# Contiguous places in memory for the triangular 64-blocks of a gated DeltaNet layer

## The chip, the cores and the metric

The kernel runs on one core of one Trainium2 chip. The metric is the device time of one launch in microseconds (us). The core has five engines that matter here: TensorE (PE, matrix products), VectorE (DVE), ScalarE (ACT), GpSimd (POOL) and SyncE (SP, which only issues transfers), and 16 DMA engines that all of them share.

## What is computed

One inference step of two layers for 512 prompt tokens and 8 sample tokens, width 2048. Layer 0 is a convolution module beside stick-breaking attention, layer 1 a gated DeltaNet with 16 query/key heads and 32 value heads of width 128. For the prompt, the DeltaNet works on chunks of 64 tokens. Per value head and chunk a unit lower triangular 64 x 64 matrix must be inverted:

```python
lmat = jnp.where(strict, jnp.einsum('bhnid,bhnjd->bhnij', kb, kc) * decay, 0.0)
tmat = lax.linalg.triangular_solve(lmat + eye, jnp.broadcast_to(eye, lmat.shape),
                                   left_side=True, lower=True, unit_diagonal=True)
u_val = tmat @ (vc * bc[..., None])
w_key = tmat @ (kb * jnp.exp(gc)[..., None])
...
def step(s, xs):
    u_n, w_n, qd_n, kd_n, a_n, gl_n = xs
    v_new = u_n - w_n @ s
    o_n = qd_n @ s + a_n @ v_new
    s = s * gl_n[..., None, None] + jnp.swapaxes(kd_n, -1, -2) @ v_new
    return s, o_n
```

## The kernel before, in words

The kernel handles the prompt in chunks of 128 tokens, so there are four chunks, and each holds two of the reference's 64-chunks. `build` (line 499) runs layer 0 first and then layer 1. Layer 1 has two stages that the change touches, and both stream the weights of the input projection through PE (`gemm`, `weights`): a block of 512 KB is loaded (`wr`, three buffers), split into a high part by ACT (`wh`) and a low part by DVE (`wl`), and multiplied.

The *preparing stage* calls `prepare(i)` (line 1307) for 16 head pairs i, some 26 us each. Each makes, for four chunks, seven 128 x 128 matrices and stores them in the DRAM tile `sp` (`spa`, line 1249; `spill[i]` is the part of head pair i): rows 0 and 1 the keys and queries, 2 the keys transposed, 3 and 4 the decayed products of both heads, and 5 and 6 the triangular matrices (`lt`) of both heads. These last two hold, on their diagonal, the two 64-blocks that have to be inverted. Then gates of some heads (`z`) are computed and stored.

`inverses(b8, iv)` (line 1377) inverts the blocks of eight head pairs at a time. The tile `m` has 128 partitions, one block of 64 x 64 on each, 2 MB in all. Eight transfers on Pool's queue (`Q2`) gather the blocks from `sp`, 16 partitions each, in rows of 64 numbers; DVE inverts them in place in some 238 operations; eight transfers scatter them back into the same places of `sp`. `inverses(0)` runs while head pairs 8 to 15 are prepared, the first half of its `m` being loaded once head pairs 0 to 3 are there. `inverses(1)` uses the same buffer for `m` and runs beside scans 0 to 7 of the next stage, in portions that `background` (line 1516) hands out.

The *scan stage* calls, for each head pair, `values(i)` (two projections and their convolution), `scan(i, ...)` (line 1594), `samples` and `normalise`. A scan loads its four chunks from `sp` into `pk` (four buffers, SP's queue), combines the two inverted 64-blocks of each head into the inverse of the 128-block with small products on PE, and runs the four steps of the recurrence.

The order of instructions on each engine is fixed by a planner, `Sched`. Every operation is recorded with its dependencies (`region`, line 120, finds out which parts of a tile two operations share) and a cost (`cost`, line 243); `flush` (line 309) simulates the engines and emits the instructions in the order of simulated start times. Pool's transfers (`GQ`) and Pool's own operations (`POOL`) are two engines for the planner but share one queue on the chip. The only operations of Pool in these stages, besides transfers, are memsets of three columns of `buf`, which the convolution (`conv_c`, line 1279) needs before ACT copies a projection from PSUM into `buf`. For a transfer the planner adds an issue time and the time of its bytes on one shared queue (lines 274, 275 and 401 to 404): 1700 ns of issue where a tile has at most 16 partitions, otherwise 340 or 560 ns, and bytes / 335 ns with a surcharge for short rows.

Of the kernel before, what the change touches and what calls it, by code (L numbers as in the profile page):

```python
# [8 lines left out]
F32 = mybir.dt.float32  # L9
# [6 lines left out]
P = 128  # L16
# [11 lines left out]
GQ = 16  # L28
# [10 lines left out]
class Sched:  # L39
# [80 lines left out]
    def region(self, ap):  # L120
        rec = self.owner.get(ap.tensor.name)
        if rec is None:
            return None
        dims, off = tuple(tuple(x) for x in ap.ap), ap.offset
        if ap.space == bass.MemoryType.DRAM:
            lo = off + sum(min(0, s * (c - 1)) for s, c in dims)
            hi = off + sum(max(0, s * (c - 1)) for s, c in dims)
            return rec, lo, hi + 1, self.parts(rec["shape"], dims, off) if len(rec["shape"]) == 4 else 1
        if ap.space == bass.MemoryType.PSUM:
            return rec, 0, P, 1  # L130
        fs = 1
        for x in rec["shape"][1:]:
            fs *= x
        key = (off % fs, dims[1:])
        m = self.masks.get(key)
        if m is None:
            idx = np.array([off % fs])
            for s, c in dims[1:]:
                if s:
                    idx = (idx[:, None] + s * np.arange(c)[None, :]).reshape(-1)  # L140
            b = np.zeros(idx.max() + 1, np.uint8)
            b[idx] = 1
            m = self.masks[key] = int.from_bytes(np.packbits(b, bitorder="little").tobytes(), "little")
        p0 = off // fs
        return rec, p0, p0 + dims[0][1], m
# [97 lines left out]
    def cost(self, eng, meth, args, kw, out, ins):  # L243

        n = self.free(out)
        PSM = bass.MemoryType.PSUM
        big = [x for x in ins if not (self.free(x) == 1 and n > 1)]
        ptr = len(ins) - len(big)
        nps = sum(1 for x in ins if x.space == PSM)
        acc = kw.get("accum_out") is not None  # L250
        if eng == "PE":
            k, m = ins[0].shape[0], out.shape[0]
            rows = 32 if k <= 32 else 64 if k <= 64 else 128
            if meth == "transpose":
                return max(109 if rows == 128 else 82, 0.833 * n + 2), (rows, 128), "t"
            if ins[1].dtype == F32R:
                return (max(120, 0.417 * n + 6) if rows == 128 else 0.833 * n + 8), (rows, 128), "r"
            cols = 32 if m <= 32 else 64 if m <= 64 else 128
            if (rows, cols) == (128, 32):
                return max(100, 1.667 * n + 52), (rows, cols), "q"  # L260
            return 2 * max(109 if rows == 128 else 58, 0.833 * n + 3), (rows, cols), "f"
        if eng == "ACT":
            f = args[2] if meth == "activation" else AF.Copy
            return 0.83 * n + (58 if nps else 109) + 93 * ptr + 105 * acc, f
        if eng in ("SP", "GQ"):
            by, run = int(4 * np.prod(out.shape)), 4096
            for x in [out] + ins:
                r = 1
                for st, c in reversed([tuple(d) for d in (x.ap if x.space == bass.MemoryType.DRAM else list(x.ap)[1:])]):
                    if st != r:  # L270
                        break
                    r *= c
                run = min(run, 4 * r)
            few = any(x.space != bass.MemoryType.DRAM and x.shape[0] <= 16 for x in [out] + ins) and by > 20000
            return (1700 if few else 340 if by / run <= 130 else 560), int(by * (1 + 77 / run if run >= 512 else 512 / max(run, 64)))
        two = sum(1 for x in big if x.space != PSM) > 1
        if eng == "DVE":
            fast = meth in ("tensor_scalar", "tensor_copy") and not nps and out.space != PSM
            if meth == "memset":
                return 0.52 * n + 60, True  # L280
            if meth == "reciprocal":
                return 6.6 * n + 70, False
            if meth == "tensor_tensor_scan":
                return 2.09 * n + 55, two
            if meth == "tensor_reduce":
                return 1.04 * self.free(ins[0]) + 65, False
            r = 0.52 if fast else 1.04
            if meth == "tensor_tensor" and n >= 100:
                inner = [[d for d in list(x.ap)[1:] if d[1] > 1] for x in big]
                if any(d and abs(d[-1][0]) > 4 for d in inner):  # L290
                    r = 1.83
            return r * n + 68 + 60 * ptr + 12 * acc, two or fast
        if meth == "tensor_tensor":
            return 1.57 * n + 430, True
        if meth == "tensor_reduce":
            return 2.1 * self.free(ins[0]) + 100, True
        if meth == "memset":
            return 0.5 * n + 130, True
        return 0.83 * n + 370 + 60 * ptr, True
# [199 lines left out]
def build(tc, a, ctx):  # L499
# [11 lines left out]
    dr = sc.pool(ctx, "dr", 1, DR)  # L511
# [736 lines left out]

    spa = dr.tile([4 * GQ, P, 7, P], F32, name="sp")
    spill = [spa[4 * i:4 * i + 4] for i in range(GQ)]  # L1250
    NZ = 7
    zd = [dr.tile([P, NT], F32, name=f"z{h}") for h in range(2 * GQ)]
    y1d = [dr.tile([P, NT], F32, name=f"y1_{h}") for h in range(NH)]
    with ExitStack() as l1:
# [52 lines left out]
        def prepare(i, lk):  # L1307
# [51 lines left out]
            for hd in range(2):  # L1359
                h = 2 * i + hd  # L1360
                gr = pm.tile([P, 4, P], F32, name="pd", bufs=1)
                PE.matmul(gr.rearrange("p c f -> p (c f)"), idr[:, h:h + 1].broadcast_to([P, P]), gst, start=True, stop=True)
                dd = lk.tile([P, 4, P], F32, name="dd", bufs=2)
                for c in range(4):
                    S.activation(dd[:, c, :], gr[:, c, :], AF.Relu, bias=gct[:, c, h:h + 1], scale=-1.0)
                S.activation(dd, dd, AF.Exp, scale=-1.0)
                it = lk.tile([P, 4, P], F32, name="it", bufs=2)
                V.tensor_tensor(it, dd, gm[:, :, 1, :], op=ALU.mult)
                Q.dma_start(sv[:, :, 3 + hd, :], it)
                lt = lk.tile([P, 4, P], F32, name="lt", bufs=2)  # L1370
                for c in range(4):
                    V.scalar_tensor_tensor(lt[:, c, :], dd[:, c, :], nb[:, c, hd:hd + 1], gm[:, c, 0, :],
                                           op0=ALU.mult, op1=ALU.mult)
                Q.dma_start(sv[:, :, 5 + hd, :], lt)


        def inverses(b8, iv):
            m = iv.tile([P, 64, 64], F32, name="m")
            blocks = []
            for i in (0, 4):  # L1380
                for blk in range(2):
                    for hd in range(2):
                        p0 = 64 * blk + 32 * hd + 4 * i
                        c0, r = 4 * (8 * b8 + i), slice(64 * blk, 64 * blk + 64)
                        blocks.append((m[p0:p0 + 16], spa[c0:c0 + 16, r, 5 + hd, r]))
            for s, dv in blocks:
                Q2.dma_start(s, dv)
            mf = m.rearrange("p j i -> p (j i)")
# [205 lines left out]
        def scan(i, vs, osb, oss, lb):  # L1594
            pk = []
            for c0 in (0, 2):
                blocks = []
                for c in (c0, c0 + 1):
                    t = lb.tile([P, 7, P], F32, name="pk", bufs=4)
                    Q.dma_start(t, spill[i][c])  # L1600
                    pk.append(t)
                    blocks += [(t, 5), (t, 6)]
                ap_ = pm.tile([64, 4, 64], F32, name="pm")
                with sc.together():
                    for q, (t, s) in enumerate(blocks):
                        PE.transpose(ap_[:, q, :], t[0:64, s, 0:64], ident[0:64, 0:64])
                at = lb.tile([64, 4, 64], F32, name="at")
                S.copy(at, ap_)
                bp = pm.tile([P, 4, 64], F32, name="pm")
                for q, (t, s) in enumerate(blocks):  # L1610
                    PE.matmul(bp[64:128, q, :], t[0:64, s, 64:128], at[:, q, :], start=True, stop=True)
                ba = lb.tile([P, 4, 64], F32, name="ba")
                S.copy(ba[64:128], bp[64:128])
                zp = pm.tile([64, 4, 64], F32, name="pm")
                for q, (t, s) in enumerate(blocks):
                    PE.matmul(zp[:, q, :], ba[64:128, q, :], t[64:128, s, 64:128], start=True, stop=True)
                for q in range(2):
                    S.copy(blocks[2 * q][0][0:64, 5:7, 64:128], zp[:, 2 * q:2 * q + 2])
# [8 lines left out]
            for c in range(4):  # L1627
                t = pk[c]
# [330 lines left out]
```

## Time and profile before

| | us |
|---|---|
| median of 3 runs | 3135.98 |
| lowest, highest | 3134.47, 3140.05 |
| the profiled execution, its own time | 3128.76 |
| its span, first to last instruction | 3127.0 |
| PE busy in the span | 3008.9 (96%) |
| DVE busy | 2312.5 (74%) |
| ACT busy | 1716.0 (55%) |
| POOL busy | 154.2 (5%) |

One execution was profiled. The preparing stage of layer 1 lies at about 1240 to 1820 us of the span, the scan stage at 1820 to 2740. In rows of instructions, `DVE m<-tmp` is an operation of VectorE that writes tile m and reads tile tmp; the line number is L433 for nearly all, because the planner emits them there, so instructions are told apart by their tiles. What stands in square brackets at the end of a row is the idle time of the engine just before it and what ended it. Transfers of SP are on the hardware queue q1, those of Pool on the software queue q0.

### The profile page before, as it was taken

To read this page: it belongs to the slowest core of one execution; us is meant where nothing else is said; L and a number is where in the kernel's file an instruction comes from. 1 tells how busy PE (TensorE), PEld (TensorE's weight loads), DVE (VectorE), ACT (ScalarE), POOL (GpSimd) and SP (SyncE) were. 2 spreads that over 40 slices of the span, in tenths; PEclk is the share of its full clock that TensorE was granted. 3 is DMA by queue.
4 is the path that set the end of the run, shared out by engine and by line. 5 is a ranking of instruction groups with operands and counts; after the bars stand their busy time and mean duration, and the time that the engine had idled before them with its cause. 6 is when DMAs were issued, how large, how long until landed. Compare 5 with 4: busy or idle time off the path is not lost.

```text
span 3127.0 us, 65405 instructions
## 1 busy us (share of the span) xinstructions
PE 3008.9 (96%) x24448; PEld 2768.6 (89%) x24448; DVE 2312.5 (74%) x5510; ACT 1716.0 (55%) x3907; POOL 154.2 (5%) x189
## 2 busy tenths in 40 slices
PE   8999999999989998999999989999998989999997
PEld 5798888888868786999999979999998889999997
DVE  2478888878764476666999949999975776765755
ACT  3256766657652266776774226555635655644544
POOL 0000000000001111000000010000000000011111
PEclk9999999999999999999999999999998999999998
DMA  9987888888967898677655385656465554576764
GB/s 319 294 279 248 299 285 287 303 292 299 305 240 268 285 307 272 164 168 149 157 148 141 119 167 160 183 147 187 133 161 158 171 149 148 149 255 191 228 182 135
DMA packets 330863, 666.99 MB, mean 213 GB/s; under 512 B 70929, under 2 KB 183570, under 8 KB 326450
## 3 DMA queue, kind: packets, MB, share of 16 engines
q1 hardware_dynamic: 327986, 654.43, 67.5%
q0 software_dynamic: 2560, 8.39, 2.3%
q8 instruction: 192, 3.15, 0.4%
q14 instruction: 125, 1.02, 0.1%
HBM read 574.95 MB, written 87.70 MB: 212 GB/s over the span
## 4 chain that ended last, share of the span: by engine, by line
PE 85%; DMA 6%; DVE 5%; ACT 1%; issue 1%; SPq 1%; POOL 0%; POOLq 0%; ACTq 0%; DVEq 0%
PE pg L433 68%; PE pm L433 9%; PE pl L433 7%; PE pd L433 2%; DMA page<-cache_k 1%; DMA m<-sp 1%; DVE wl L433 1%; DMA wa<-w_ada 1%; DMA S<-state_delta 1%; DVE acc L433 1%; DVE junk L433 1%; DVE S L433 1%; SPq L433 0%; DVE page L433 0%; DMA pk<-sp 0%
## 5 line engine op out<-in xcount | busy, mean ns | idle before, releaser
L433 PE MATMUL pg<-uh,wh 128*128 128x260 f32 (+1 forms) x6112 | 1336.3, 288 | 13.1 <-ACT wh L433 5.1
L433 PE MATMUL pg<-ul,wh 128*128 128x260 f32 (+1 forms) x6112 | 1334.0, 288 | 3.6 <-DVE ul L433 3.5
L433 PEld LDWEIGHTS pg<-uh,wh 128*128 128x128 f32 (+1 forms) x6112 | 998.0, 190 | 67.1 <-issue 45.9
L433 PEld LDWEIGHTS pg<-ul,wh 128*128 128x128 f32 (+1 forms) x6112 | 995.6, 190 | 43.9 <-issue 32.6
L433 PE MATMUL pg<-uh,wl 128*128 128x260 f32 (+1 forms) x6112 | 878.7, 287 | 0.0
L433 DVE TENSOR_TENSOR wl<-wr,wh 128x1024 fp32r<-128x1024 f32 (+3 forms) x508 | 615.2, 1211 | 315.8 <-ACT wh L433 149.3
L433 ACT CAST wh<-wr 128x1024 fp32r<-128x1024 f32 (+3 forms) x508 | 511.2, 1007 | 600.4 <-PE pg L433 495.3
L433 PEld LDWEIGHTS pg<-uh,wl 128*128 128x128 f32 (+1 forms) x6112 | 788.3, 189 | 42.1 <-issue 38.4
L433 DVE TENSOR_TENSOR tmp<-m 128x224 f32<-128x224 f32 (+19 forms) x238 | 201.1, 845 | 4.0
L433 DVE SCALAR_TENSOR_TENSOR acc<-gp,conv_w_a,acc 128x512 f32<-128x512 f32 x240 | 181.4, 756 | 4.1 <-ACT acc L433 0.9
L433 ACT ACTIVATE page<-page 128x128 f32<-128x128 f32 x512 | 151.1, 297 | 42.7 <-DVE page L433 38.2
L433 ACT ACT_TABLE_LOAD x125 | 160.4, 1283 | 12.6 <-DVE rs L433 8.9
L433 DVE SCALAR_TENSOR_TENSOR cacc<-buf,conv_w_c,cacc 128x512 f32<-128x512 f32 x192 | 143.1, 746 | 11.5 <-ACT cacc L433 10.0
L433 DVE TENSOR_REDUCE m<-tmp 128x32 f32<-128x224 f32 (+19 forms) x238 | 131.0, 551 | 4.0
L433 DVE SCALAR_TENSOR_TENSOR junk<-page,qbc 128x128 f32<-128x128 f32 x512 | 115.8, 290 | 14.0 <-DMA page<-cache_k 9.5
L433 ACT ACTIVATION_READ_ACCUMULATOR page<-page 128x1 f32 x512 | 96.2, 188 | 0.0
L433 PE MATMUL pl<-wa,cpad 128*32 128x512 f32 x512 | 83.3, 605 | 4.5 <-DMA wa<-w_ada 4.3
L433 DVE TENSOR_TENSOR page<-page,qbc 128x1024 f32<-128x1024 f32 x64 | 78.7, 1230 | 6.2 <-DMA page<-cache_k 6.2
L433 PE MATMUL pg<-yh,wh 128*128 128x260 f32 x320 | 79.2, 283 | 0.0
L433 PE MATMUL pg<-yl,wh 128*128 128x260 f32 x320 | 79.2, 283 | 0.0
L433 DVE SCALAR_TENSOR_TENSOR S<-S,egb,pl 128x128 f32<-128x128 f32 x256 | 71.8, 340 | 8.9 <-PE pl L433 8.6
L433 PE MATMUL pl<-page,wst 128*32 128x512 f32 x512 | 72.3, 604 | 1.5 <-DMA page<-cache_v 1.5
(386 smaller groups left out, 3531.1 us busy)
## 6 DMA issues: line engine op xcount, KB each, us to landing
wr<-w_in_odd SPq DMA_DIRECT2D x194, 512.0 KB, 4.8
page<-cache_k SPq DMA_DIRECT2D x128, 512.0 KB, 5.4
wa<-w_ada SPq DMA_DIRECT2D x128, 512.0 KB, 5.4
page<-cache_v SPq DMA_DIRECT2D x128, 512.0 KB, 5.9
wr<-w_out_odd SPq DMA_DIRECT2D x128, 512.0 KB, 3.8
wr<-w_in_even SPq DMA_DIRECT2D x94, 512.0 KB, 5.0
page<-w_ada SPq DMA_DIRECT2D x128, 256.0 KB, 5.4
pk<-sp SPq DMA_DIRECT2D x64, 448.0 KB, 3.9
```

What stands on the lines that cost most here:

```text
L433: o[2](*o[3], **o[4])
```

## The change

Two DRAM tiles `tri0` and `tri1` are added, one for the upper and one for the lower 64-block of each 128-chunk, in which each block of 64 x 64 is one contiguous run of 16 KB.

- `prepare` stores, besides the whole `lt`, its two diagonal blocks into them: two more transfers on SP for each of two heads, 64 KB each, 64 in all.
- `inverses` loads `m` from them and stores it back in four transfers of 32 partitions each instead of eight of 16, all contiguous. All four loads span eight head pairs. The inverted blocks are no longer written into `sp`.
- `scan` loads a chunk as before, which now brings the blocks as they were before the inversion, and then lays the inverted ones over it: two more transfers on Pool's queue for each of the 64 chunks, 32 KB each, in rows of 64 numbers, 128 in all.
- Two lines of the planner change: `region` looks for shared parts by shape rather than by the number of dimensions, and the issue time of 1700 ns is given only to transfers with rows under 512 bytes.

```diff
@@ region
-            return rec, lo, hi + 1, self.parts(rec["shape"], dims, off) if len(rec["shape"]) == 4 else 1
+            return rec, lo, hi + 1, self.parts(rec["shape"], dims, off) if rec["shape"][2:] == [7, P] else 1
@@ cost
-            few = any(x.space != bass.MemoryType.DRAM and x.shape[0] <= 16 for x in [out] + ins) and by > 20000
+            few = any(x.space != bass.MemoryType.DRAM and x.shape[0] <= 16 for x in [out] + ins) and by > 20000 and run < 512
@@ build
+    tri = [dr.tile([2, 4 * GQ, 64, 64], F32, name=f"tri{j}") for j in range(2)]
@@ prepare
                 Q.dma_start(sv[:, :, 5 + hd, :], lt)
+                for j in range(2):
+                    r = slice(64 * j, 64 * j + 64)
+                    Q.dma_start(tri[j][hd, 4 * i:4 * i + 4].rearrange("c p f -> p c f"), lt[r, :, r])
@@ inverses
-            for i in (0, 4):
-                for blk in range(2):
-                    for hd in range(2):
-                        p0 = 64 * blk + 32 * hd + 4 * i
-                        c0, r = 4 * (8 * b8 + i), slice(64 * blk, 64 * blk + 64)
-                        blocks.append((m[p0:p0 + 16], spa[c0:c0 + 16, r, 5 + hd, r]))
+            for blk in range(2):
+                for hd in range(2):
+                    p0 = 64 * blk + 32 * hd
+                    blocks.append((m[p0:p0 + 32], tri[blk][hd, 32 * b8:32 * b8 + 32]))
@@ scan
                     Q.dma_start(t, spill[i][c])
+                    for j in range(2):
+                        r = slice(64 * j, 64 * j + 64)
+                        Q2.dma_start(t[r, 5:7, r], tri[j][:, 4 * i + c].rearrange("h p f -> p h f"))
                     pk.append(t)
```

## Rows read from the trace of the kernel before

**Rows 1.** The page's chain that ended last, by engine and by line

```profile
PE 85%; DMA 6%; DVE 5%; ACT 1%; issue 1%; SPq 1%; POOL 0%; POOLq 0%; ACTq 0%; DVEq 0%
PE pg L433 68%; PE pm L433 9%; PE pl L433 7%; PE pd L433 2%; DMA page<-cache_k 1%; DMA m<-sp 1%; DVE wl L433 1%; DMA wa<-w_ada 1%; DMA S<-state_delta 1%; DVE acc L433 1%; DVE junk L433 1%; DVE S L433 1%; SPq L433 0%; DVE page L433 0%; DMA pk<-sp 0%
```

**Rows 2.** The chain in order of time: start us, us, what

```profile
1457.21 11.46 DMA m<-sp
...
1817.35 10.60 DMA z<-dd
...
1833.23 20.51 DMA m<-sp
...
2334.38 11.72 DMA pk<-sp
```

**Rows 3.** Windows: stretch, us, busy PE PEld DVE ACT POOL, PEclk, DMA share, GB/s

```profile
1460.00:1480.00 20.00, 15.26 (x105) 15.04 (x104) 11.04 (x39) 7.46 (x11) 0.10 (x1) 0.83 0.79 152
1820.00:1840.00 20.00, 16.65 (x137) 16.23 (x136) 7.11 (x14) 6.93 (x15) 6.63 (x12) 1.00 0.86 149
1840.00:1860.00 20.00, 10.21 (x83) 9.80 (x81) 5.76 (x17) 2.79 (x5) 0.10 (x1) 0.84 1.01 195
1860.00:1880.00 20.00, 18.70 (x144) 16.40 (x145) 16.57 (x42) 9.25 (x27) 0.20 (x2) 0.81 0.62 182
...
1860.00:2340.00 480.00, 476.08 (x4063) 458.79 (x4064) 449.02 (x1068) 261.26 (x652) 7.98 (x27) 0.99 0.58 161
2340.00:2360.00 20.00, 15.45 (x114) 13.81 (x113) 4.49 (x10) 5.97 (x18) 0.00 (x0) 0.83 0.89 253
```

**Rows 4.** Timeline at the border, 1799 to 1862: start us, us, engine, instruction, idle before

```profile
1799.45 6.05 POOL L433 DMA_DIRECT2D sp<-m  x8 [169.11 <-DVE m L433]
1826.82 0.77 POOL L433 DMA_DIRECT2D m<-sp  x1 [21.31 <-DMA wr<-w_in_odd]
1828.02 0.31 ACT L433 ACTIVATE selr<-ct 128x128 fp32r<-128x128 f32 x1 [10.70 <-DMA z<-dd]
1853.96 0.11 DVE L433 MEMSET m<- 128x64 f32 x1 [14.36 <-DMA m<-sp]
1861.30 1.12 PE L433 MATMUL pm<-ct,vc 128*128 128x128 f32 x4 [9.31 <-ACT vc L433]
```

**Rows 5.** Timeline at the start of the first inversion

```profile
1468.88 0.11 DVE L433 MEMSET m<- 128x64 f32 x1 [6.22 <-DMA m<-sp]
1472.19 0.58 PE L433 MATMUL pm<-kql,kqh 128*128 128x256 f32 x1 [4.75 <-DVE kql L433]
```

**Rows 6.** DMA queues, 1799 to 1826, then 1455 to 1470: packets, MB, share of 16

```profile
q0 software_dynamic: 640, 2.10, 63.0%
q1 hardware_dynamic: 776, 2.37, 22.8%
...
q0 software_dynamic: 320, 1.05, 65.1%
q1 hardware_dynamic: 1082, 1.42, 35.4%
```

**Rows 7.** DMA issues of the whole span: count, KB each, median us to landing

```profile
pk<-sp SPq DMA_DIRECT2D x64, 448.0 KB, 3.9
...
m<-sp POOLq DMA_DIRECT2D x16, 256.0 KB, 9.8
...
kw<-krd SPq DMA_DIRECT2D x16, 16.0 KB, 2.3
```

**Rows 8.** Timeline at the end of the second inversion and about scan 10

```profile
2318.36 1.52 POOL L433 DMA_DIRECT2D sp<-m  x2 [24.76 <-DVE m L433]
...
2428.84 0.32 SPq L433 DMA_DIRECT2D pk<-sp  x1
2442.01 0.41 PE L433 MATMUL pm<-ct,pk 64*64 64x64 f32 x4 [0.51 <-ACT pk L433]
2444.21 0.10 POOL L433 MEMSET buf<- 128x3 f32 x1 [41.31 <-DVE cacc L433]
```

## The prediction

> **What bounds the kernel now.** I read the page first. TensorE (PE) makes up 85% of the chain that ended last [rows 1]. On that chain one DMA of this change stands out: the load of m from sp, 1.0% or some 31 us, with the load of pk from sp below it [rows 1]. The chain in order of time shows where: 11.5 us at 1457, 20.5 us at 1833 (behind a z store of 10.6 us), and 11.7 us of pk at 2334 [rows 2]. These are the start of the first inversion, the border between the preparing stage and the scan stage together with the start of the second inversion, and the end of the second inversion with scan 8 behind it. The windows say what PE lost there [rows 3]: 20 - 15.26 = 4.7 us idle in 1460 to 1480; 3.35 + 9.79 + 1.30 = 14.4 us in 1820 to 1880; 4.55 us in 2340 to 2360. After each the granted clock is down for a while (a mean of 0.83, 0.81 and 0.83 of full speed, so part of the stretch was at 1.2 instead of 2.4 GHz): 0.17 x 20 = 3.4 us, 0.19 x 20 = 3.8 us (3.1 without what fell on idle time), 3.4 us. All that this layout of memory costs today is so about 8 + 17.5 + 8 = 33 us. Between these places PE is full: 476.1 of 480 us from 1860 to 2340 [rows 3], so what is gained at the border stays gained. In that stretch VectorE is nearly full as well (449 us), with the same work before and after.
>
> **Why those waits are long.** At the border Pool issues eight stores of m in 6.05 us, and then stands until 1826.8 before the first load of m for the second inversion, because m may be overwritten only when the stores have landed: 27.4 us. VectorE then stands 14.36 us until 1853.96 for that load, another 27 us, and PE 9.31 us for a product of VectorE that is queued behind. ScalarE stands 10.70 us for the z store [rows 4]. The queues say why: the software queue moved 2.10 MB in 63.0% of 27 us, so 17.0 us of all 16 DMA engines, while the hardware queue moved 2.37 MB in 22.8%, 6.2 us [rows 6]. That is 8.1 against 2.6 us per MB. The first goes through pieces of 64 numbers (256 B) on the DRAM side, the second mostly through long rows.
>
> **The change, part by part.** *Stores and loads of m become contiguous.* A pass of 2.10 MB would cost 5.5 us of the engines at the hardware queue's price. The fixed remainder of today's pass is 27.4 - 17.0 - 6.2 = 4.2 us; with as many other transfers beside it a new pass takes 4.2 + 5.5 + 6.2 = 15.9 us, with the same share of them (x = 4.2 + 5.5 + 0.23x) 12.6 us. I take 14. The price could also stay as it is (17.0, no gain), if not the pieces but the software queue were slow.
>
> The Trainium skill's page "DMA: Bandwidth & Descriptors" (section Specifications) gives 512 B as the least size for full rate and read-modify-write below it. Its fit in "Anatomy of one DMA" gives 2.0 us plus bytes at 436 GB/s, by which 2.10 MB would be an estimated 6.8 us alone; no run here shows this pass alone, and the sum goes by the rows.
>
> *The border.* Store and load end 54.5 - 28 = 26.5 us earlier. The order of instructions is fixed by the planner, which will move VectorE's first operation on m forward as well. From its cost lines (274, 401 to 404) it believes in 8 x 1.76 + 0.65 + 2.35 = 17.1 us for a pass today, and in 0.40 + 0.65 + 4 x 1.60 = 7.4 us for the new one: 2 x 9.7 = 19.4 us forward for two. The wait of 14.4 us so becomes 14.4 - (26.5 - 19.4) = 7.3 at worst, nothing at best. Of today's 14.36 us PE felt 9.31, so the first 5 are covered, and I charge PE 2. The z store, issued at 1817.35 [rows 2], finds the software queue empty (1799.45 + 14 = 1813.5), so ScalarE's wait and the weights behind it go. Gain: 14.4 + 3.1 - 2 = **15.5 us** (10 to 17.5). Next late would be scan 0's pk with its overlays, which are not yet needed at that time.
>
> *The first inversion.* Today half of m is loaded early; after the change each of the four loads spans eight head pairs and waits for the last of them, so 2.10 MB come at once where 1.05 MB came. Today these take 65.1% of 15 us, 9.8 us, beside 5.3 us of others [rows 6], and VectorE waits 6.22, PE 4.75 us [rows 5]. New: 5.5 us (at 2.6 per MB) to 7.8 us (at 3.7, this stretch's price), plus some 1.5 us for the small stores in front. That ends 0.5 to 2.8 us earlier, while the planner moves VectorE's operation 10.0 - 7.4 = 2.6 us forward. Between a gain of 4 and a loss of 2 I take **1 us lost**.
>
> *The end of the second inversion.* pk no longer waits for it and can be loaded long before; the overlay waits in its place. Store 14 us, then three Pool issues at 0.76 us (6.05 / 8) [rows 4] and one landing of 4 us: 20 us, against 27.7 us today, from the first store at 2318.4 [rows 8] to the end of pk's wait at 2346.1. By the planner the same path falls from 21.5 to 11.5 us. The stall is moved forward by some 8 us rather than removed; the products that stood before it move behind it, where the scans have gaps. Between 0 and 8 us I take **3 us gained**.
>
> *Added: 64 small stores on SP, 128 overlays on Pool.* Each side moves 4.2 MB in 256 B pieces; at 8.1 us per MB that is 34 us of engine time, 2.1 us in each of 16 preparations and of 16 scans, where the DMA share is 0.79 and 0.58 [rows 3]. On SP they stand ahead of later weight loads, which have three buffers. An overlay's price is not in the trace: from issue to landing between 2.3 us (16 KB on SP) and 9.8 us (256 KB on Pool) [rows 7]; I take 4, nearer the small transfer, as 32 KB are 0.3 us of the engines. It lies in cover: a chunk issued at 2428.84 lands after 3.9 us (median) [rows 7] and is used at 2442.01 [rows 8], 9.3 us later, against 2 x 0.76 + 4 = 5.5 us. That is about the shortest cover of the ordinary scans. Pool waits for a chunk's landing, and behind it stand the memsets of buf, for which ScalarE's copies out of PSUM wait; the memset at 2444.21 [rows 8] comes after that chunk's overlays would be done. If a weight load or a memset is late, it costs PE directly: 0 to 8 us in all; I take **2 us lost**.
>
> **Sum:** 15.5 - 1 + 3 - 2 = 15.5 us. The profiled span of 3127.0 us becomes 3111.5, and its own time of 3128.8 becomes 3113.3. The median of the runs is 7.2 us above the profiled one, so the forecast is **3120 us**.
>
> **Rivals.** *The stalls re-form (no change).* The planner moves the first use of m forward by as much as the transfers gain, since it believes in cheaper transfers than the chip gives: only the z store's wait (3.3 us) and some clock go, 4 to 6 us in all, 3131 us. For it: in both stalls of today the plan was short by 4 to 10 us a pass. Against: at the border two passes gain 7 us more than the plan moves. The same time results if the software queue, not the pieces, sets the price. Chance 0.17.
>
> *The overlays come late (slower).* From the eight stores of today in 27.4 us, 3.4 us each in sequence, four overlays of a chunk pair would take 13.7 us, 4.4 above the cover of 9.3. Scans 8 to 15 have little else for PE, and 8 x 4.4 = 35 us would be added, 3155 us with the gain of 15.5 off. It decides from a lag of 9.3 us on. For it: everything goes through Pool in order. Against: 32 KB are an eighth of the bytes. Chance 0.12.
>
> The Trainium skill's page "SBUF — State Buffer" (SBUF: two separate sides) speaks for this rival: a DMA issued from Pool has its descriptors written by Pool, and VectorE in a two-port mode shuts Pool out meanwhile. The trace has no sign of it in Pool's issues, 0.76 us both at 1799 and at 1827, but these rows don't tell what VectorE did meanwhile. If it held, the times would be those of this rival.
>
> **How the numbers follow.** About 0.2% (6.3 us) is what a measurement here can tell. Forecast 0.68 (3104 to 3130), no change 0.17 (3131), slower 0.12 (3155), 0.03 for a reordered plan that does better than the bounds. The range takes in the forecast's bounds (gains of 10 to 17.5, -2 to 4, 0 to 8, 0 to -8) and the no-change case: 3104 to 3136. Faster 0.71, same 0.17, slower 0.12.
>
> **What would show it.** Right: between 1790 and 1880 no wait of VectorE for m above 7 us, PE idle under 4 us, the software queue's share far below 63%, Pool's wait between store and load near 10 us instead of 21. At the end of the second inversion pk is loaded early, and PE waits for a tri overlay instead. Wrong: PE waits for pk<-tri in many scans, ScalarE's buf copies wait for Pool, or PE waits for late weights in the preparations.

## The result and the profile after

| | before | after |
|---|---|---|
| median of 3 runs, us | 3135.98 | 3094.34 |
| lowest, highest | 3134.47, 3140.05 | 3093.54, 3099.93 |
| ratio (95% interval) | | 0.9883 (0.9864 to 0.9902) |
| profiled span, us | 3127.0 | 3097.8 |

The change makes the kernel 41.6 us faster by these medians, 33.0 us in the repetition below (3131.89 to 3098.91 us, ratio 0.9895, 0.9874 to 0.9916), and 29.2 us by the two profiled spans. The profiled execution was 7.2 us below its median before and is 5.6 us above it after, which is nearly all of the difference between 41.6 and 29.2. The forecast was 15.5 us with a lower end of 3104 us: the direction was right, the size was not.

The page's chain of the changed kernel, by line, answers to [rows 1]: neither the load of m nor pk is among its largest entries any more, and PE's share is about the same.

```profile
PE 83%; DVE 7%; DMA 6%; ACT 1%; issue 1%; SPq 1%; POOLq 0%; POOL 0%; ACTq 0%; DVEq 0%
PE pg L433 66%; PE pm L433 8%; PE pl L433 6%; PE pd L433 2%; DMA S<-state_delta 2%; DMA wa<-w_ada 1%; DVE wl L433 1%; DMA page<-cache_k 1%; DVE acc L433 1%; DVE junk L433 1%; DMA o_ds<-S 1%; DVE page L433 1%; DVE blk L433 1%; SPq L433 0%; DVE tmp L433 0%
```

In order of time, the answer to [rows 2], the chain still holds one load of m, at the first inversion, with the landing of a small store just ahead of it (start us, us, what). At the border a z store is still on it, as before; at the border and at the second inversion's end no transfer of m, `tri` or pk is.

```profile
1448.43 5.90 DMA tri<-lt
...
1456.62 12.28 DMA m<-tri
...
1821.88 9.11 DMA z<-dd
```

The windows answer to [rows 3]; columns as there.

```profile
1460.00:1480.00 20.00, 13.38 (x91) 13.18 (x90) 11.05 (x37) 6.60 (x9) 0.10 (x1) 0.75 0.65 162
1820.00:1840.00 20.00, 18.42 (x154) 18.21 (x153) 8.95 (x25) 7.52 (x17) 1.84 (x6) 1.00 0.98 250
1840.00:1860.00 20.00, 19.56 (x172) 17.54 (x171) 19.13 (x52) 8.04 (x18) 3.65 (x8) 1.00 0.71 217
1860.00:1880.00 20.00, 20.00 (x173) 19.73 (x174) 19.55 (x45) 11.96 (x33) 1.27 (x3) 1.00 0.36 101
```

At the border, 1820 to 1880, PE now stands 1.58 + 0.44 = 2.0 us where it stood 14.4, and the clock stays at full speed. At the first inversion, 1460 to 1480, it stands 6.6 us where it stood 4.7, with a lower clock.

The timeline at the border answers to [rows 4].

```profile
1801.62 1.93 POOL L433 DMA_DIRECT2D tri<-m  x4 [166.32 <-DVE m L433]
1816.37 2.05 POOL L433 DMA_DIRECT2D m<-tri  x4 [12.82 <-DMA wr<-w_in_odd]
...
1831.05 0.31 ACT L433 ACTIVATE selr<-ct 128x128 fp32r<-128x128 f32 x1 [9.20 <-DMA z<-dd]
...
1832.60 0.11 DVE L433 MEMSET m<- 128x64 f32 x1 [0.59 <-issue]
...
1834.33 0.51 PE L433 MATMUL pg<-uh,wh 128*128 128x260 f32 x2 [1.58 <-ACT wh L433]
```

The store of m takes 14.75 us until the first load may be issued, where it took 27.4, and VectorE finds m loaded. The second inversion so starts at 1832.6 instead of 1854.0.

That is the part that was forecast. The rest is not in any of the places of [rows 3]. A scan begins with small transposes of its blocks on PE (`pm<-ct,pk`). The next answers take the windows from the first transposes of one scan to those of the next, scans 7 to 11, and count only the products of the projections (tile pg). Columns: stretch, its length, PE busy with them and their number, granted clock, DMA share, GB/s. Before:

```profile
2229.30:2345.00 115.70, 100.69 (x774) 1.00 0.57 146
2345.00:2393.90 48.90, 26.91 (x168) 0.82 0.58 178
2393.90:2438.80 44.90, 31.98 (x192) 0.86 0.43 140
2438.80:2485.80 47.00, 31.35 (x192) 0.93 0.52 166
2485.80:2529.30 43.50, 15.99 (x101) 0.84 0.48 143
```

After:

```profile
2234.80:2295.00 60.20, 48.77 (x344) 1.00 0.62 176
2295.00:2349.10 54.10, 41.96 (x250) 0.84 0.67 192
2349.10:2396.60 47.50, 37.38 (x251) 1.00 0.66 185
2396.60:2446.00 49.40, 36.50 (x244) 0.97 0.52 150
2446.00:2495.40 49.40, 35.99 (x234) 0.93 0.55 175
```

Before, 774 products were run between scans 7 and 8, while scan 8 waited for the second inversion, and only 653 were left for scans 8 to 11. After, 344 are run there and 979 (978 when none is counted twice) in scans 8 to 11. These four scans took 184.3 us and take 200.4: they do 325 products more in 16.1 us more. With PE full, 4063 matrix instructions took 480 us [rows 3], some 0.12 us each, so 325 products are 39 us of work, 23 us more than the added time. Of these, 16 us went into time in which PE had stood idle (21.8 us before, 5.6 after); the rest fits the higher clock. All of PE's work in those scans shows it, first before, then after:

```profile
2345.00:2529.30 184.30, 162.52 (x1229) 148.76 (x1229) 125.86 (x368) 104.95 (x290) 0.60 (x6) 0.86 0.51 158
```

```profile
2295.00:2495.40 200.40, 194.79 (x1575) 184.12 (x1576) 138.22 (x395) 115.39 (x307) 21.30 (x44) 0.93 0.60 176
```

PE stood 21.8 us of 184.3 at a mean clock of 0.86, and stands 5.6 us of 200.4 at 0.93. From the first transposes of scan 0 to those of scan 12 the changed kernel needs 641.6 us instead of 663.5, for nearly the same number of products (3495 and 3492). Those 21.9 us were forecast as 3, less 2 for the overlays.

### The profile page after: what moved, and what is told of

Its sections match the earlier page's. It is cut to its first block, busy times and chain, and to the rows that moved or that the text cites. A ratio compares the mean times of both kernels' runs of the same rounds, so it can differ in the third digit from the quotient of the medians.

```text
span 3097.8 us, 65898 instructions
## 1 busy us (share of the span) xinstructions
PE 3005.4 (97%) x24448; PEld 2764.8 (89%) x24448; DVE 2311.0 (75%) x5510; ACT 1716.6 (55%) x3907; POOL 211.7 (7%) x301
## 4 chain that ended last, share of the span: by engine, by line
PE 83%; DVE 7%; DMA 6%; ACT 1%; issue 1%; SPq 1%; POOLq 0%; POOL 0%; ACTq 0%; DVEq 0%
PE pg L433 66%; PE pm L433 8%; PE pl L433 6%; PE pd L433 2%; DMA S<-state_delta 2%; DMA wa<-w_ada 1%; DVE wl L433 1%; DMA page<-cache_k 1%; DVE acc L433 1%; DVE junk L433 1%; DMA o_ds<-S 1%; DVE page L433 1%; DVE blk L433 1%; SPq L433 0%; DVE tmp L433 0%
## 5 line engine op out<-in xcount | busy, mean ns | idle before, releaser
L433 POOL DMA_DIRECT2D pk<-tri x128 | 74.9, 590 | 451.7 <-PE pm L433 153.5
```

Of the source, the lines that this page charges most:

```text
L433: o[2](*o[3], **o[4])
```

## The experiments

Three theories were set against each other. **A:** the part that was missed is the products. While scan 8 waits for the end of the second inversion, PE runs projections of later head pairs, and these are then missing between the dependent steps of scans 8 to 11. **B:** only the waits on the transfers count, and the smooth scans 8 to 11 are an accident of one profile. **C:** the planner's new order makes the gain, not the faster transfers. All ratios are against the kernel before on the same chip.

### The changed kernel again

No edit.

> The changed kernel once more, unchanged, for a second profile and a second interval beside the other runs on this chip. Both theories: 35 to 45 us below the kernel before. Theory A (where the gain lies): of it some 16 us at the border of the stages, and 15 to 25 us in scans 8 to 11, where PE had gaps before and has none now. Theory B (the waits on the DMAs alone): the smooth scans 8 to 11 belong to one profile by chance, and a second profile shows gaps in them again.

Measured: 3098.91 us against 3131.89, ratio 0.9895 (0.9874 to 0.9916). That is 33.0 us, just under the 35 to 45 expected. The second profile has the same products (344, then 978), as it must, since the program fixes the order. PE stands 5.1 us in scans 8 to 11, and they take 195.1 us. The smooth scans are no accident; B falls in that part.

### The pace of the second inversion, both ways

```diff
-                background(6000)
+                background(8500)
```

> The kernel before with one number changed: the second inversion is handed out in portions of 8500 instead of 6000 per scan, so that little of it is left when scan 8 is due. No transfer and no memory place is changed. Theory A (scan 8 waits for the end of the second inversion, PE runs projections of later heads meanwhile, and these are then missing between the steps of scans 8 to 11): the stretch between the first transposes of scans 7 and 8 shrinks from 116 us to 60 to 80, the gaps and the low clock of scans 8 to 11 go, and the kernel is 12 to 25 us faster than before, with the border's stall of 14 us still there. Theory B (only waits on the transfers cost): within 5 us of the kernel before.

Measured, in the kernel before: 3125.33 us against 3131.89, ratio 0.998 (0.9967 to 0.9993). The stretch from scan 7 to 8 shrinks to 95 us only and holds 628 products; scans 8 to 11 hold 706 and PE still stands 16.6 us in them. That is 6.6 us (2 to 10 by the interval), where A expected 12 to 25 and B under 5. The edit was weaker than expected: the inversion ends at 2310 instead of 2316. VectorE was nearly full before (449 of 480 us in [rows 3]), which may be why; it was not tested. From scan 0 to 12 the run needs 654.0 instead of 663.5 us, so the gain follows what moved, but as a test of A it decides little.

```diff
-                background(6000)
+                background(4000)
```

> The changed kernel with the second inversion handed out in portions of 4000 instead of 6000 per scan, so that it ends later; all transfers as in the changed kernel. Theory A: the stretch between scans 7 and 8 grows from 60 us to over 90, gaps come back in scans 8 to 11, and it is 12 to 25 us slower than the changed kernel. Theory B: within 5 us of the changed kernel.

Measured, in the changed kernel: 3106.41 us, ratio 0.9913 (0.9891 to 0.9936), 7.5 us above the changed kernel's run on that chip. The inversion ends at 2303 instead of 2275, the stretch from scan 7 to 8 grows from 60 to 86 us and from 344 to 508 products, 852 are left, and PE stands 8.1 us in scans 8 to 11. The direction is A's, but the size is below the 12 to 25 us that were expected, and the two intervals overlap.

### The planner's costs and the transfers, one without the other

In the changed kernel, high costs for the planner, meant as the old ones:

```diff
+            if eng == "GQ" and by == 4 * 32 * 64 * 64:
+                return 2 * 1760 - 60, 6 * by // 2
```

> The changed kernel, but the planner is told the old cost for the loads and stores of m (each of the four counts as two of the old ones, 3.5 us of issue and its bytes times three), so that the order of instructions expects them late, while on the chip they are as fast as in the changed kernel. Theory C (the gain is the planner's new order, not the faster transfers): the gain is lost, 0 to 10 us below the kernel before. Theory A: the border's stall does not come back, since the data is there before its use, at least 15 us below the kernel before; the end of the second inversion is planned some 10 us later for scan 8, which costs up to 10 us against the changed kernel.

Measured: 3103.19 us, ratio 0.9903 (0.9876 to 0.9931), 28.7 us below the kernel before and 4.3 above the changed one. The edit goes further than the old costs. By line 275, rows of 256 B count their bytes twice, not three times, so that eight old transfers are 8 x 1.76 + 0.65 + 1.57 = 16.3 us for the planner, the four of the changed kernel are 7.4, and the four of this run are 3.52 + 0.65 + 4 x 4.70 = 23.0 (lines 401 to 404). The run so is no test of the old order; it shows that the gain stays when the planner takes the transfers for slower than ever, so it does not need the low costs.

In the kernel before, new costs for the planner:

```diff
+            if eng == "GQ" and by == 4 * 16 * 64 * 64:
+                return 140, by + by // 53
```

> The kernel before with all its transfers, but the planner is told that a load or store of m costs what four contiguous ones cost (two of the eight count as one of the four), so that the order of instructions expects the data early while the chip delivers it late. Theory C (the gain is the new order): 10 us or more below the kernel before. Theory A (it is the transfers): no gain; VectorE waits for m longer than today's 14.4 us at the border and 6.2 us in the first inversion, 0 to 15 us slower than before.

Measured: 3132.39 us against 3132.84, ratio 1.0007 (0.9992 to 1.0023). The order alone gains nothing in sum, but not because nothing changes. At the border VectorE waits 23.27 us for m, and PE all but stops; the windows of this run, columns as in [rows 3]:

```profile
1840.00:1860.00 20.00, 0.84 (x7) 0.62 (x6) 0.00 (x0) 0.00 (x0) 0.00 (x0) 0.65 0.94 124
1860.00:1880.00 20.00, 15.13 (x106) 14.79 (x106) 18.50 (x40) 7.09 (x11) 0.10 (x1) 0.76 0.60 180
```

In exchange the inversion ends 15 us after the first transposes of scan 7 instead of 86, and the products lie as in the changed kernel. Tile pg, from scan 7 to 8 and from scan 8 to 12:

```profile
2279.30:2344.00 64.70, 48.27 (x328) 0.95 0.70 187
2344.00:2533.00 189.00, 148.87 (x994) 0.99 0.55 165
```

Scans 8 to 11 do 341 products more than before in 4.7 us more, with 2.7 us of PE idle. So the gaps there close without any faster transfer once the inversion is ordered to end early, and that is worth 12.3 us from scan 0 to 12 (651.2 us, before 663.5). It is paid ahead of scan 0, which comes 628.5 us after the first store of the preparing stage instead of 614.2. In scans 0 to 6 PE idles more too (12.6 us, before 1.9). This speaks for A's mechanism and against C as the cause of the sum.

### Half of the change each

Contiguous load, but scattered store and no overlay:

```diff
             for s, dv in blocks:
                 Q2.dma_start(s, dv)
+            blocks = []
+            for i in (0, 4):
...
+                        blocks.append((m[p0:p0 + 16], spa[c0:c0 + 16, r, 5 + hd, r]))
...
-                    for j in range(2):
-                        r = slice(64 * j, 64 * j + 64)
-                        Q2.dma_start(t[r, 5:7, r], tri[j][:, 4 * i + c].rearrange("h p f -> p h f"))
```

> Half of the change: the blocks are stored contiguously in the preparations and loaded contiguously into m, but the inverted ones are scattered back into sp by eight transfers as before, and a scan loads them with its chunk, without overlays. Theory A: the second inversion starts some 13 us earlier (one contiguous pass of two), its end follows by 10 to 20 us, scan 8 still waits 25 us for the scattered store and its chunk, part of the gaps in scans 8 to 11 stays; 8 to 20 us below the kernel before. Theory B: only what the border gains, 5 to 9 us.

Measured: 3111.46 us against 3132.84, ratio 0.9935 (0.9914 to 0.9957), 21 us. This run has the products of e4 in every scan (328, then 994), so the two can be compared as the same order with slow and fast loads: 3132.39 and 3111.46 us. VectorE's wait for m at the border is 10.80 us instead of 23.27, and the way from the start of the preparing stage to scan 0 is 614.1 us instead of 628.5. PE idles 13.0 us in scans 0 to 6 here too. Against the kernel before nothing is gained ahead of scan 0 (614.1 and 614.2 us); the gain lies from scan 0 to 12, 642.7 us instead of 663.5.

Gathered load, but contiguous store and overlays (the small stores in `prepare` left out):

```diff
-            for s, dv in blocks:
-                Q2.dma_start(s, dv)
+            for i in (0, 4):
...
+                        Q2.dma_start(m[p0:p0 + 16], spa[c0:c0 + 16, r, 5 + hd, r])
```

> The other half: m is gathered from sp by eight transfers as before (without the extra stores in the preparations), but stored back contiguously into the new places, and the scan lays the inverted blocks over its chunks. Theory A: the border gains the z store's wait and one pass of two, scan 8 follows the end of the second inversion by 15 us instead of 28, so that the gaps in scans 8 to 11 shrink; 15 to 28 us below the kernel before. Theory B: 8 to 12 us below.

Measured: 3113.8 us, ratio 0.9942 (0.992 to 0.9965), 19 us. The inversion ends 63 us after scan 7, 483 products lie between scans 7 and 8, 862 in scans 8 to 11, where PE idles 9.3 us. Ahead of scan 0 this half gains 3.7 us (610.5), from scan 0 to 12 it gains 19.6 (643.9). Each half brings more than B allows, and nearly all of it lies in the scans, not at the border.

### Two head pairs' gates moved back into their scans

```diff
-        early = [(8 + j) for j in range(4)]
+        early = [(8 + j) for j in range(2)]
```

> The kernel before with one number changed: the z projections of head pairs 10 and 11 are no longer computed ahead during scans 0 to 7 but in their own scans; nothing of the inversions or of memory is changed. It puts 4 x 48 products of 260 columns per head pair into scans 10 and 11, which had 192 and 101 in the kernel before. Theory A (PE's gaps in scans 8 to 11 are missing products, since the chain of a scan of some 45 us has place for 240 of them): the gaps of scans 10 and 11 fill, 5 to 14 us below the kernel before. Theory B: within 5 us of it.

Measured: 3166.76 us against 3132.84, ratio 1.0115 (1.0093 to 1.0138): 34 us slower, where A as put there expected a gain. The expectation was wrong about where the products go. The gaps of scans 10 and 11 did fill (253 and 272 products), but the products are missing elsewhere: 667 instead of 774 lie between scans 7 and 8, none in scan 8, 101 in scan 9. The plan gives PE whatever may run while scan 8 waits; which projections moved, the trace doesn't tell. From scan 7 to 8, then scans 8 to 11, then scans 12 to 14 together, tile pg:

```profile
2230.20:2338.70 108.50, 88.28 (x667) 0.97 0.56 149
2338.70:2384.90 46.20, 0.00 (x0) 0.50 0.39 120
2384.90:2437.40 52.50, 20.53 (x101) 0.66 0.39 115
2437.40:2484.30 46.90, 37.72 (x253) 1.00 0.51 147
2484.30:2533.20 48.90, 39.08 (x272) 1.00 0.55 165
...
2533.20:2721.90 188.70, 160.86 (x1141) 1.00 0.50 147
```

Scans 12 to 14 of the kernel before:

```profile
2529.30:2689.10 159.80, 130.84 (x907) 1.00 0.54 158
```

This is the clearest reading of A's mechanism. Scan 8 takes 46.2 us with no product, at a mean clock of 0.50; scan 10 takes 46.9 with 253, at 1.00; scan 9, with 101 at 0.66, takes 52.5. So 253 products lie in a scan here at next to no cost. In scans 12 to 14, where PE was nearly full before (159.7 of 159.8 us), 234 products more cost 28.9 us, 0.12 us each. From scan 0 to 12 the run does 244 products fewer than the kernel before and yet needs 3.6 us more (667.1 us).

### The first inversion

In the changed kernel, the four loads of the first inversion are planned longer, at 23.0 us by the costs of e3 (eight old ones were 16.3):

```diff
+            if eng == "GQ" and by == 4 * 32 * 64 * 64 and out.space != bass.MemoryType.DRAM:
+                self.loads += 1
+                if self.loads <= 4:
+                    return 2 * 1760 - 60, 6 * by // 2
```

> The changed kernel, with one cost in the planner corrected: the four loads of m of the first inversion alone are planned as long as eight old ones (3.5 us of issue each, bytes times three), near to the 14 us that they take on the chip. Expected from e3, where the same cost left PE idle for 1.7 instead of 7.0 us between 1455 and 1490 and took the low clock there and around 1674 away: 6 to 12 us below the changed kernel, if what the change loses at the first inversion is VectorE standing before data that the plan believes landed. If that loss is the transfers' own (2 MB at once), no more than 2 us.

Measured: 3088.34 us against 3130.86, ratio 0.9871 (0.9853 to 0.9889). The window of the first inversion and one of the stretch where the changed kernel stood a second time (16.82 of 20 us busy from 1660 to 1680 there, 18.25 in the kernel before):

```profile
1460.00:1480.00 20.00, 18.30 (x147) 17.57 (x146) 18.22 (x50) 14.39 (x23) 0.10 (x1) 1.00 0.63 165
...
1660.00:1680.00 20.00, 20.00 (x168) 19.80 (x167) 19.65 (x26) 8.71 (x11) 0.00 (x0) 1.00 0.65 194
```

PE idles 1.7 us instead of 6.6, at full clock, and the stall at 1674 is gone. The transfers are the same, only the order of the instructions is another. The loss there is the plan's, as expected, since a longer planned load takes it away. At the border 8.5 us of idle time come back: VectorE waits 13.0 us for m there, and PE 8.3 us of it behind `wl`. The run is 10.6 us below the changed kernel by the medians and 8 by the ratios; the two ran on different chips, and the intervals overlap. Between the first store of the preparing stage and scan 0, where the edit acts, its profile gains 4.6 us (598.3 against 602.9). Single profiles differ by as much elsewhere: the stretch before that store, 7236 products in every run, takes 1247.1 us here and 1250.8 to 1258.1 in the others.

In the changed kernel, the loads of m cut into halves again:

```diff
-            for s, dv in blocks:
-                Q2.dma_start(s, dv)
+            for i in (0, 16):
+                for s, dv in blocks:
+                    Q2.dma_start(s[i:i + 16], dv[i:i + 16])
```

> The changed kernel, but m is loaded in eight contiguous transfers of 16 partitions, of which the first four need head pairs 0 to 3 (8 to 11) alone, as in the kernel before. Expected: 1.05 MB instead of 2.10 MB are left when the first inversion is due, VectorE's wait falls to 2 to 5 us; 2 to 8 us below the changed kernel. If only the plan matters there, VectorE is planned forward by as much and nothing is gained.

Measured: 3101.31 us, ratio 0.9903 (0.9886 to 0.9919), no gain on the changed kernel. PE still idles 5.0 us at the first inversion, and VectorE waits 6.32 us for m, above the 2 to 5 expected. At the border PE idles 8.6 us, where the z store lands late behind the eight loads.

### Overlays on SP

```diff
-                        Q2.dma_start(t[r, 5:7, r], tri[j][:, 4 * i + c].rearrange("h p f -> p h f"))
+                        Q.dma_start(t[r, 5:7, r], tri[j][:, 4 * i + c].rearrange("h p f -> p h f"))
```

> The changed kernel with the 128 overlays issued on SP instead of Pool. Expected by the theory that the overlays are hidden behind the cover of a chunk: within 5 us of the changed kernel. If Pool's descriptors are held up by VectorE, the overlays land earlier than the median of the changed kernel and scans get shorter, 5 us or more below it. If SP stands before each chunk's landing, weight loads queue behind and it is slower by 10 us or more.

Measured: 3114.72 us, ratio 0.9954 (0.9938 to 0.997), some 16 us above the changed kernel's run on the other chip. SP's own waits from 1860 to 2700 begin with one that the changed kernel's do not have there (engine, what it waits for: us, count, longest):

```profile
SPq L433 <- DMA pk<-sp: 126.6, 52, 5.6
SPq L433 <- PE pl L433: 101.2, 33, 11.9
```

PE idles 13.4 us in scans 0 to 6, where it idles 5.4 with the overlays on Pool. That SP's waits hold up weight loads is not shown: no engine waits for a weight load in these scans. The edit also gave the planner another order (337 products between scans 7 and 8, the inversion's end 11 us after scan 7), and e4 and e6, which have no overlays at all, idle as long there (12.6 and 13.0 us). What makes this run slower was not isolated.

The issue rows of the overlays (engine, count, KB, median us to landing) are, for the changed kernel and for this run:

```profile
pk<-tri POOLq DMA_DIRECT2D x128, 32.0 KB, 3.0
```

```profile
pk<-tri SPq DMA_DIRECT2D x128, 32.0 KB, 2.3
```

Both lie far below the cover of 9.3 us of [rows 8], and the longest landing from Pool, 8.0 us, is below it too. The rule of the Trainium skill's page "SBUF — State Buffer" (SBUF: two separate sides), by which VectorE in a two-port mode can shut Pool out from writing descriptors, does not show in these medians, 3.0 against 2.3 us, though VectorE is busy 93% of the time from 1860 to 2340; whether it was in that mode, the trace doesn't tell.

### The pace on top

```diff
-                background(6000)
+                background(7000)
```

> e10 with the second inversion handed out in portions of 7000 instead of 6000. The runs so far order themselves by how long after scan 7 the second inversion ends: 87 us in the kernel before, 69, 63, 38 in the changed one, 16 where scans 8 to 11 had no gaps left, but scans 1 to 7 had some. Expected: it ends 20 to 35 us after scan 7, scans 8 to 11 lose up to 5 us less and scans 1 to 7 some more; within 5 us of e10.

Measured, e10 with this edit: 3089.48 us, ratio 0.9864 (0.9846 to 0.9882), the same as e10. The inversion ends 15 us after scan 7, where 20 to 35 were expected. Scans 8 to 11 have 1.8 us of idle time left, scans 0 to 6 have 10.5 instead of 5.2.

### All runs side by side

From the traces: how long after the first transposes of scan 7 the second inversion's last reduction ends (a closing memset, which the store waits for, follows 1 to 7 us later), products from scan 7 to 8 and from 8 to 12, and PE's idle time and mean clock in scans 8 to 11.

| run | inversion's end, us | products 7 to 8 | products 8 to 12 | idle, us | clock |
|---|---|---|---|---|---|
| before | 86 | 774 | 653 | 21.8 | 0.86 |
| e9 | 78 | 667 | 625 | 23.5 | 0.79 |
| e1 | 69 | 628 | 706 | 16.6 | 0.87 |
| e2 | 69 | 508 | 852 | 8.1 | 0.92 |
| e7 | 63 | 483 | 862 | 9.3 | 0.92 |
| after, a0, e10, e5 | 38 | 344 | 978 | 4.1 to 5.6 | 0.93 to 0.96 |
| e3 | 25 | 320 | 1020 | 5.7 | 0.98 |
| e6 | 16 | 328 | 994 | 2.9 | 1.00 |
| e4 | 15 | 328 | 994 | 2.7 | 0.99 |
| e11 | 15 | 336 | 1004 | 1.8 | 1.00 |
| e8 | 11 | 337 | 994 | 6.1 | 0.96 |

The later the inversion ends, the more products are run ahead of scan 8, the fewer are left, and the longer PE stands in scans 8 to 11. The relation holds roughly with old and new transfers and with changed costs; e1 and e2 differ by half at the same end, and e8 stands a little out of it. It has another side: the runs with the earliest ends, e3, e4, e6, e8 and e11, idle 10.5 to 13.5 us in scans 0 to 6, where the changed kernel idles 5.4. VectorE does more of the inversion in these scans (204 operations in e6, 194 in the changed kernel, 186 before); that this is the reason was not tested.

## Why the prediction was wrong

**The border: right.** 15.5 us were forecast from the idle time of 14.4 us and the clock. Measured: idle 2.0 us, full clock, so 12.4 + 3.1 = 15.5 us. The wait between store and load is 14.75 us; 14 were taken. That the sum is met to the tenth is in part luck. The 2 us were charged for VectorE's wait, which is gone (0.59 us); the 1.58 us that PE stands come from ScalarE's `wh`, behind the z store, whose wait was to go and is 9.2 us of 10.7. The gain hangs on the plan as well: in e10, with the same transfers, PE stands 8.5 us there. And by line 275 the planner's pass today is 16.3 us, not 17.1 (see e3), so the worst case of VectorE's wait was 5.7 us, not 7.3. The parts of the pass came out differently too. The queues from the first store to the end of the load, 1801 to 1816 and 1816 to 1831, against [rows 6]:

```profile
q0 software_dynamic: 192, 2.10, 66.5%
q1 hardware_dynamic: 439, 1.43, 24.9%
...
q0 software_dynamic: 192, 2.10, 61.3%
q1 hardware_dynamic: 547, 1.61, 34.1%
```

A pass still takes 0.665 x 15 = 10.0 us of the DMA engines, 4.8 us per MB, between the scattered 8.1 and the hardware queue's 2.6 from which I took 5.5. The sign that the software queue's share would be far below 63% so did not come; its time fell from 17.0 us to 10.0 instead. The Trainium skill's fit in "DMA: Bandwidth & Descriptors" (Anatomy of one DMA), an estimated 6.8 us for a pass alone, is below that too; here other transfers ran beside it.

**The first inversion: the right sign, too small.** 1 us lost was taken and 2 was the bound. Idle time grows from 4.7 to 6.6 us and the clock's loss from 0.17 x 20 = 3.4 to 0.25 x 20 = 5.0, and the idle time in 1660 to 1680 grows from 1.75 to 3.2 us. From the first store of the preparing stage to scan 0 the change gains 11.3 us (614.2 to 602.9); as what is left of the border's 15.5, this place costs some 4. Two terms were too small. The small stores in front were to cost 1.5 us, and the last of them is 5.90 us of the chain; 2.10 MB were to take 5.5 to 7.8 us, and the load is 12.28 us of the chain. VectorE's first operation on m so comes at 1469.1 us, not earlier than before (1468.9). e10 shows the other part: with VectorE's instruction planned later, the loss goes, which is the mechanism that was named.

**The end of the second inversion: the step that failed.** I took 3 us, between 0 and 8. The range was made from the stall in 2340 to 2360 and its clock alone, with the sentence that the products in front would "move behind it, where the scans have gaps" as a remark without a price. It was the largest term of all. The four scans behind had 21.8 us of idle time and a clock of 0.86 in the same trace, the windows were there to be read, and I did not count them into the bound. What ended the kernel's time there was not the wait for pk but the products that the wait had used up. Measured, scans 0 to 11 gain 21.9 us with the overlays' cost in it: PE idles 13.2 us there instead of 28.1, and the rest fits the clock. The path behind the inversion shrank by 12 us (from the first store to scan 8's first transposes 14.5 us instead of 26.6), where the prediction had 8. But the inversion itself also ends earlier, which the prediction had not, since it took VectorE's work in that stretch as the same. Its last reduction comes 43 us earlier (2273 against 2316), its first store 38 us. Some 21 of the 43 are the earlier start (1832.6 against 1854.0). In the other 21, VectorE's operations on m take 165 us in both kernels, but between the inversion's first operation and its last reduction stand 16 us less of other work and 5 us less idle time; the splitting of weights is 3.5 us of that (54 blocks against 57). Why the plan comes out so was not isolated.

**The overlays and small stores: 2 us were too many.** An overlay lands after 3.0 us (median, 4 taken), and the trace shows no wait of PE for one; PE stands 1.8 us before scan 8, which the trace puts to no transfer. In the preparing stage PE is busy 200.0 of 200 us from 1260 to 1460 in both profiles, with the 64 small stores and without.

**The rivals.** The slower one did not come: the lag on Pool is 3.0 us in the median and 8.0 at most, under the 9.3 from which it would have decided. Its price took scans 8 to 15 as short of other work; scans 12 to 14 are full before the change (159.7 of 159.8 us). The stalls re-formed in one of three places, the first inversion. What came is nearest to the case that was given 0.03, a reordered plan that does better than the bounds.

In sum: 11.3 us up to scan 0 (15.5 at the border less some 4 at the first inversion) and 21.9 in scans 0 to 11 are 33.2 us; from scan 12 to the end the profiles differ by 4.7 us the other way, which leaves 28.5 of the 29.2 measured in the spans. Of the 4.7, 3.6 us lie between scans 12 and 15, where 18 products more are run (925 against 907).

**What stays open.** Which of the planner's decisions ends the inversion 38 us after scan 7 in the changed kernel, 25 with the high costs (e3) and 63 with gathered loads (e7) was not isolated; e4 and e6 show that the planned length of the load is one of them. How the 21.9 us divide between the earlier start, the shorter inversion and the shorter path behind it is open too. The runs' medians differ by 33 and 42 us and the profiles by 29 to 33, so some us of the gain lie within the runs' own spread; all are far above the 15.5 forecast.

## What to carry to other kernels

Where a chain of dependent steps leaves gaps, independent work that lies in reserve is worth as much as the gaps that it would fill. A wait that PE "covers" with such work isn't free: count what is left for the stretch behind it, and read that stretch's idle time and clock into the bound. And where instructions stand in an order that was planned with costs, a cost that is too low for the first user of a transfer brings a stall back that the faster transfer had removed: e10, which tells the planner a longer time, is some 8 us faster by the ratios, and its profile shows 4.6 us of that in the stage with the edit.

## What was not expected of the hardware

In e9 a scan with no product at a mean clock of 0.50 took as long as one with 253 at 1.00 (46.2 and 46.9 us); one with 101 at 0.66 took 52.5. A contiguous store of m on Pool's queue took 4.8 us of the engines per MB, nearly twice the 2.6 of the hardware queue's transfers beside it (24.9% of 15 us for 1.43 MB). The same 32 KB overlay landed after 3.0 us from Pool and 2.3 us from SP, yet the run with SP was some 16 us slower; why is open.
